# A fused decoder layer: wide GpSimd products go to VectorE, the second norm's scale leaves the up projection, the branch operands are split in steps

## The chip, the cores and the metric

The kernel runs on one core of one Trainium2 chip. The metric is the device time of one execution in microseconds (us). The engines are TensorE (PE in the profile, with its weight loads as PEld), VectorE (DVE), ScalarE (ACT), GpSimd (POOL) and SyncE (SP), whose queue issues nearly all DMA transfers. Each engine runs its own instructions strictly in order and waits on semaphores for the others.

## The reference, cut to what matters

One decoder layer for 1024 prompt tokens and 8 x 4 sample tokens (1056 columns together), width 1024, all float32:

```
xn = rms_norm(x, norm1_g)
z  = xn @ w_in                       # q, k, v and gates of three mixers, and three branch gates
o_a, o_b, o_c = GLA scan, FoX attention, HGRN2 scan   # o_a and o_c: rms_norm(o) * silu(gate)
merged = sum_b sigmoid(g_b) * (o_b @ w_branch_b)
x  = x + merged @ w_out
h  = rms_norm(x, norm2_g)
x  = x + (silu(h @ w_ffn_gate) * (h @ w_ffn_up)) @ w_ffn_down
y  = rms_norm(x, final_norm_g)       # rms_norm(x, g) = x * rsqrt(mean(x*x) + EPS) * g
```

States of the two scans and the new attention keys and values are outputs too.

## The kernel before

Activations lie with features on the 128 partitions and the 1056 columns along the free dimension. So a "wide" tile is 128 x 1056 (528 KB). Each float32 operand of a matmul is split into a rounded part and its remainder (`x` and its subtracted low part, `wh` and `wl`): ACT writes the rounded part (L110, L223), DVE subtracts (L111, L224), and PE multiplies three of the four combinations.

The stages, in the order of the trace: the first norm (0 to 85 us); the input projection in pairs of feature rows by seven products each with 264-column matmuls (L1914; 85 to 690), where the FoX attention runs in the background; the rest of the input projection with 352-column matmuls (L139; to about 985), where the two scans run in the background; 24 branch jobs (to about 1150), in the order FoX, GLA, HGRN2, eight rows each; eight output jobs (to 1250); the up projection `ffn_up` in 22 pairs (to 1700); the down projection (to 1900) and the last norm.

Background work is a set of Python generators in four queues (`bg3`, `bgs`, `bg4`, `bgn`). `tick` is called after every third matmul of a job and advances one queue by one step, in turn. `drain` runs queues to their end. All of this only decides the order in which instructions are written; the compiler's scheduler may then move instructions of one engine past each other where data allow it.

A branch job `n` (0 to 23) loads its gate from DRAM (`z_dram`), ACT applies the sigmoid (L1591), PE multiplies four operand tiles in three column chunks of 12 matmuls each, and DVE multiplies each chunk by the gate (L1596 for the first eight, L1598 after them). Three PSUM banks (`pg`) take the chunks in turn, so PE can be three chunks ahead of DVE. From the ninth job on POOL adds the chunk into `merged` (L1599). Two things stand between these jobs. `ranges`, written ahead of job number `AHEAD`, drains the background queues and tests a flag in an `If` (L1536, L1537) that every engine passes; its body recomputes the scans in another way and isn't executed here. Behind it the four scan outputs for the next eight jobs are fetched (`fetch_o`) and split, two in front of each of the next two jobs (`halves`).

`head_norm` (L1112 to L1133) normalises a scan's output of one head: an Ln and an Exp on ACT (L1116, L1117), three DVE instructions of a Newton step, one product by the head's scale, one by the gate (L1130, on POOL).

In `ffn_up` an even pair is the gate projection `z`, an odd pair the up projection `y`. `post` computes `z*r1`, the sigmoid `g`, `g*r1`, `z*g` and `y*z` (L1972), where `r1` is the second norm's factor for each column; of each two tiles the first is on DVE and the second on POOL. `r1` comes from `rstd`, called as a whole in the first pair. The weights of each pair are added and split by DVE (L1804 to L1808, L224), and chunks leave PSUM by ACT (L1925) or DVE (L1923).

Of the kernel before, what the change touches and what calls it, by code (L numbers as in the profile page):

```python
# [8 lines left out]
F32 = mybir.dt.float32  # L9
# [12 lines left out]
CW = 352  # L22
# [18 lines left out]
AHEAD = 5  # L41
# [49 lines left out]
class Body:  # L91
    def __init__(self, nc, tc, A, O):
        self.nc, self.tc, self.A, self.O = nc, tc, A, O

        self.bg, self.bg3, self.bg4, self.bgs, self.bgn = [], [], [], [], []
        self.turn = 0
        self.early = []
# [131 lines left out]
    def rstd(self, out, sqs, scale, n=NT):  # L229
# [3 lines left out]
        for sl in self.chunks():  # L233
            sl = slice(sl.start, min(sl.stop, n))
            w = sl.stop - sl.start
            ps = self.pm.get()
            for i, sq in enumerate(sqs):
                nc.tensor.matmul(ps[:, :w], self.ones, sq[:, sl], start=i == 0, stop=i == len(sqs) - 1)
            nc.vector.tensor_scalar(v[:, sl], ps[:, :w], scale, EPS, ALU.mult, ALU.add)
            self.pm.put(ps)  # L240
        yield
        nc.scalar.activation(t[:, :n], v[:, :n], AF.Ln)
        nc.scalar.activation(out[:, :n], t[:, :n], AF.Exp, scale=-0.5)
        for sl in self.chunks():
            sl = slice(sl.start, min(sl.stop, n))
            self.newton(out[:, sl], v[:, sl], t[:, sl])
        self.u.put(v, t)
# [32 lines left out]
    def run(self):  # L280
# [17 lines left out]
        self.lf_dram = dp.tile([4, NT], F32, name="lf_dram")  # L298

# [251 lines left out]
    def in_pairs(self, job, nxt):  # L551
# [13 lines left out]
        def post(n, y):  # L565

            name = PAIRS[2 * n][0]
            e = nc.vector, nc.gpsimd
# [9 lines left out]
            for i in range(2):  # L578
                if name == "gq":
                    nc.vector.scalar_tensor_tensor(y[i], y[i], 0.125, self.r1, ALU.mult, ALU.mult)  # L580
                else:
                    e[i].tensor_tensor(y[i], y[i], self.r1, ALU.mult)  # L582
            yield
            yield
            if name in ("gr", "hq", "hg"):
                for i in range(2):
# [3 lines left out]
                    e[i].tensor_tensor(y[i], y[i], g, ALU.mult)  # L590
# [507 lines left out]
    def head_norm(self, o, gate, gn, dst, done):  # L1098
# [17 lines left out]
        nc.scalar.activation(t[:, :n], v[:, :n], AF.Ln)  # L1116
# [13 lines left out]
        nc.gpsimd.tensor_tensor(o[:, :n], o[:, :n], v, ALU.mult)  # L1130
# [114 lines left out]
    def scan_mul(self, hf, q, k, qe, ke):  # L1245
        nc = self.nc
        tt = slice(hf * 512, hf * 512 + 512)
        nc.gpsimd.tensor_tensor(ke, ke, k[:, tt], ALU.mult)
        nc.gpsimd.tensor_tensor(qe, qe, q[:, tt], ALU.mult)
# [168 lines left out]
    def scan_sample(self, q, k, b, vn, hs, os, s0_src, sts_out, done):  # L1418
# [77 lines left out]
        nc.gpsimd.tensor_tensor(S0, S0, ebl, ALU.mult)  # L1496
# [54 lines left out]
    def out_jobs(self, last):  # L1551
# [32 lines left out]
        def branch_job(n):  # L1584
            bi, f = order[n]

            def begin():
# [3 lines left out]
                self.sig = nc.scalar.activation(gates[n], gates[n], AF.Sigmoid)  # L1591

            def evac(ps, c, sl):
# [3 lines left out]
                else:  # L1597
                    nc.vector.tensor_tensor(g[:, sl], ps, g[:, sl], ALU.mult)  # L1598
                    nc.gpsimd.tensor_tensor(mg[:, sl], mg[:, sl], g[:, sl], ALU.add)  # L1599
# [32 lines left out]
        held = []  # L1632

        def ranges():
# [3 lines left out]
            held[:] = fetch_o(0)  # L1638

        def halves(bi, h0):  # L1640
            for h in (h0, h0 + 1):
                split_o(bi, h, held[h])
# [39 lines left out]
    def wout_jobs(self, M):  # L1682
# [24 lines left out]
        def end(f, hh, xf):  # L1707
# [3 lines left out]
            else:  # L1711
                nc.scalar.activation(xf, hh, AF.Square)
                nc.gpsimd.tensor_tensor(self.r1, self.r1, xf, ALU.add)
# [164 lines left out]
    def pair_run(self, nxt, phase, post, hook, into=None, beside=None):  # L1878
# [15 lines left out]
        for n in range(self.pairs):  # L1894
# [3 lines left out]
            y = into(n) if into else [self.u.get(), self.u.get()]  # L1898
# [60 lines left out]
            if post:  # L1959
                assert not pend  # L1960
                steps = post(n, y)
                if steps is not None:
                    next(steps)
                    pend.append(steps)
# [5 lines left out]
    def ffn_up(self, job, nxt):  # L1970
        nc = self.nc
        TT = lambda e, o, x, y, op=ALU.mult: e.tensor_tensor(o, x, y, op)  # L1972
        V, P = nc.vector, nc.gpsimd
# [3 lines left out]
        def phase():  # L1977
            self.close("o")
            f = self.open("f", "right", reuse_waits="tile")
            self.u = Slots(f, 6, [128, NT], F32, "fu")  # L1980
# [6 lines left out]

        def hook(n, k):
            if n == 0 and k == 1:
                for _ in self.rstd(self.r1, [self.r1], 0.125):  # L1990
                    pass
            if n < N - 1:
                return

            if k == 1:
# [9 lines left out]
            elif k == 6:  # L2005
                for j in range(2):
                    take(loads.pop(0))

# [322 lines left out]
```

## Time and profile before

| | us |
|---|---|
| median of 3 runs (lowest to highest) | 1962.71 (1962.51 to 1969.71) |
| the profiled execution | 1971.27 |
| its span in the trace | 1969.5 |
| mean granted TensorE clock, share of full speed | 0.987 |

The profile is of an execution of its own, a little longer than the three timed ones; 1.8 us lie outside its span. Its rows give when an instruction started, how long it took, and what ended the idle time in front of it. "PEclk" is the share of full speed that the clock of TensorE was granted in a stretch; its two levels are 0.5 (1.2 GHz) and 1.0 (2.4 GHz), and a value between them is a mean.

### The profile page before, as it was taken

What the parts mean: (1) busy time and instruction counts of PE and PEld (TensorE: products, weight loads), DVE (VectorE), ACT (ScalarE), POOL (GpSimd) and SP (SyncE); (2) the same over time, 40 slices, a digit from 0 to 9 for tenths busy, and PEclk for the clock granted to TensorE, in tenths of its full rate; (3) what the DMA queues carried; (4) which work ended last, traced back from release to release, by engine and by line L of the source; (5) the groups of instructions that cost most, each with busy time, mean ns of one, the idle gap of its engine ahead of it and who ended that gap; (6) DMA issues with size and microseconds to landing.
All of it is one profiled execution on the core that took longest, in us unless ns stands there. A gap on an engine that the chain in (4) does not pass through costs nothing. (4 is left out here: it accounts for less than half of the span.)

```text
span 1969.5 us, 37117 instructions
## 1 busy us (share of the span) xinstructions
PE 1909.6 (97%) x14846; PEld 1818.4 (92%) x14846; DVE 1338.5 (68%) x2205; ACT 826.0 (42%) x1464; POOL 463.5 (24%) x295
## 2 busy tenths in 40 slices
PE   8999999999999999999989999999999999999997
PEld 6889999999999988888889999999999999999896
DVE  8866556644666577786565555977677777668965
ACT  5444444322433354454544423633334333332435
POOL 5211011211222132122113522222223222110004
PEclk9999999999999999999999999999999999999998
DMA  3433433577666534343446443122221221423212
GB/s 145 150 128 113 155 102 94 157 235 239 191 207 204 179 109 143 121 144 122 144 151 223 147 148 114 62 76 99 76 76 66 77 99 52 175 87 110 85 60 88
DMA packets 96983, 253.60 MB, mean 129 GB/s; under 512 B 14562, under 2 KB 28066, under 8 KB 96802
## 3 DMA queue, kind: packets, MB, share of 16 engines
q1 hardware_dynamic: 95250, 249.96, 37.3%
q8 instruction: 118, 1.93, 0.4%
q10 hardware_dynamic: 1296, 0.67, 0.1%
q14 instruction: 63, 0.52, 0.1%
q0 software_dynamic: 256, 0.52, 0.1%
HBM read 183.74 MB, written 67.37 MB: 127 GB/s over the span
## 5 line engine op out<-in xcount | busy, mean ns | idle before, releaser
L139 PE MATMUL pg<-x,wh 128*128 128x352 f32 x1692 | 431.3, 336 | 9.2 <-DVE u L1596 7.2
L1914 PE MATMUL pg<-x,wh 128*128 128x264 f32 x2080 | 400.1, 288 | 8.1 <-POOL frmul L773 2.7
L1914 PEld LDWEIGHTS pg<-x,wh 128*128 128x128 f32 x2080 | 322.9, 188 | 14.7 <-POOL x L224 2.9
L139 PEld LDWEIGHTS pg<-x,wh 128*128 128x128 f32 x1692 | 297.4, 191 | 31.4 <-issue 14.7
L1914 PE MATMUL pg<-x,wl 128*128 128x264 f32 x1040 | 295.7, 284 | 0.4 <-DVE wl L224 0.4
L139 PE MATMUL pg<-x,wl 128*128 128x352 f32 x846 | 277.4, 328 | 1.4 <-PEq L1537 1.4
L1914 PEld LDWEIGHTS pg<-x,wl 128*128 128x128 f32 x1040 | 195.7, 188 | 0.6 <-DVE wl L224 0.6
L1914 PE MATMUL pg<-x,rh 128*128 128x264 f32 x976 | 187.3, 288 | 2.3 <-DVE fu L1923 2.3
L139 PEld LDWEIGHTS pg<-x,wl 128*128 128x128 f32 x846 | 162.2, 192 | 2.2 <-issue 2.2
L1914 PE MATMUL pg<-pr,wh 128*128 128x264 f32 x832 | 162.5, 293 | 0.0
L1914 PEld LDWEIGHTS pg<-x,rh 128*128 128x128 f32 x976 | 152.4, 190 | 4.0 <-DVE fu L1923 2.7
L224 DVE TENSOR_TENSOR wl<-wf,wh 128x512 fp32r<-128x512 f32 (+2 forms) x125 | 108.6, 870 | 54.0 <-ACT wh L223 50.3
L223 ACT ACTIVATE wh<-wf 128x512 fp32r<-128x512 f32 (+2 forms) x125 | 77.5, 620 | 153.4 <-PE pg L1914 120.7
L1914 PE MATMUL pg<-x,rl 128*128 128x264 f32 x488 | 139.2, 285 | 0.0
L1914 PEld LDWEIGHTS pg<-pr,wh 128*128 128x128 f32 x832 | 129.9, 190 | 4.7 <-issue 3.1
L582 POOL TENSOR_TENSOR pu<-pu,r 128x1056 f32<-128x1056 f32 x21 | 59.0, 2809 | 312.1 <-ACT pu L1925 312.1
L1914 PE MATMUL pg<-pr,wl 128*128 128x264 f32 x416 | 118.8, 286 | 0.0
L1972 POOL TENSOR_TENSOR fu<-fu,r 128x1056 f32<-128x1056 f32 x22 | 67.1, 3048 | 216.1 <-ACT fu L1925 202.9
L110 ACT ACTIVATE wh<-wf 128x1024 fp32r<-128x1024 f32 (+2 forms) x60 | 51.3, 855 | 151.2 <-PE pg L139 135.9
L1914 PEld LDWEIGHTS pg<-x,rl 128*128 128x128 f32 x488 | 92.4, 189 | 0.0
L1923 DVE TENSOR_TENSOR pu<-pu,pg 128x264 f32<-128x264 f32 x132 | 55.3, 426 | 53.4 <-PE pg L1914 52.1
L1925 ACT ACTIVATE pu<-pg 128x264 f32<-128x264 f32 x176 | 66.3, 381 | 58.8 <-PE pg L1914 54.0
(510 smaller groups left out, 4371.0 us busy)
## 6 DMA issues: line engine op xcount, KB each, us to landing
z_dram<-pu SPq DMA_DIRECT2D x44, 528.0 KB
wf<-in_wgu SPq DMA_DIRECT2D x44, 512.0 KB
u<-z_dram SPq DMA_DIRECT2D x39, 528.0 KB
wf<-in_winp SPq DMA_DIRECT2D x30, 512.0 KB
fa<-in_kc SPq DMA_DIRECT2D x48, 256.0 KB
fa<-in_vc SPq DMA_DIRECT2D x48, 256.0 KB
wf<-in_win SPq DMA_DIRECT2D x19, 512.0 KB
a_dram<-fu SPq DMA_DIRECT2D x18, 528.0 KB
```

Source lines behind the costliest of these rows:

```text
L110: nc.scalar.activation(wh[:, :n], wf[:, :n], AF.Copy)
L139: nc.tensor.matmul(ps[:m, :CW], a[:, k, :], b[:, sl], start=n == 0, stop=n == 3 * job.kt - 1)
L223: nc.scalar.activation(h, x, AF.Copy)
L224: (eng or nc.vector).tensor_tensor(l, x, h.bitcast(F32), ALU.subtract)
L582: e[i].tensor_tensor(y[i], y[i], self.r1, ALU.mult)
L1914: nc.tensor.matmul(ps, a[:, w], b, start=first and m == 0, stop=m == 3 * K - 1, skip_group_check=not first)
L1923: nc.vector.tensor_tensor(out, out, ps, ALU.add)
L1925: nc.scalar.activation(out, ps, AF.Copy)
L1972: TT = lambda e, o, x, y, op=ALU.mult: e.tensor_tensor(o, x, y, op)
```

## The change

1. Wide element products and sums that POOL executed go to DVE: the input projection's norm product and sigmoid product (L582 x21, L590 x6), the gate product of `head_norm` (L1130 x8), the scans' decay products (L1248 and L1249 x12 each) and state product (L1496 x6), the branch sum (L1599 x48), the sum of squares (L1713 x7), all of `post` in `ffn_up` (L1972 x43) and the differences of the down projection (L2070 x6, L2082 x6).
2. The up projection is no longer multiplied by `r1`: `g*r1` (44 products) is gone. Instead the residual `h` is divided by it. `rstd_2` loads each of the eight `h` tiles from DRAM in the background of `ffn_up`, multiplies it by `v*r1` (which is 1/r1) and stores it, and it stores `EPS*v` (`v_dram`), which the last norm adds in place of `EPS`. The Newton step works on whole tiles, and the second norm's steps come one per product of the up projection.
3. `fetch_o` and the splits of the branch operands become `load_o`, a generator in `bgn`: it fetches four tiles, waits eight steps, and splits one tile per step. `drain` in front of jobs 8 and 16 finishes it. `AHEAD` goes from 5 to 6, and `tick` skips one call after each step when only one queue holds work.
4. `head_norm` asks for the table set of Ln and Exp once (`tables`) when a sigmoid has been issued since.
5. In the last up pair `y*z` and its split are spread over the last products; `ffn_up` has 8 buffers in place of 6, the down projection 14 in place of 13.

```diff
-AHEAD = 5
+AHEAD = 6
...
     def tick(self):
         qs = self.bg3, self.bgs, self.bg4, self.bgn
-        for _ in () if self.cold else qs:
-            q = qs[self.turn % 4]
+        if self.cold or not any(qs):
+            return
+        if self.pause:
+            self.pause -= 1
+            return
+        while not qs[self.turn % 4]:
             self.turn += 1
-            if q:
-                self.pump(q)
-                return
+        self.pump(qs[self.turn % 4])
+        self.turn += 1
+        self.pause = max(0, 2 - sum(map(bool, qs)))
...
+    def rstd_2(self):
+        nc = self.nc
+        v, t = self.u.get(), self.u.get()
+        for sl in self.chunks():
+            ps = self.pm.get()
+            nc.tensor.matmul(ps[:, :CW], self.ones, self.r1[:, sl], start=True, stop=True)
+            nc.vector.tensor_scalar(v[:, sl], ps[:, :CW], 0.125, EPS, ALU.mult, ALU.add)
+            self.pm.put(ps)
+            yield
+        r = self.r1
+        nc.scalar.activation(t, v, AF.Ln)
+        nc.scalar.activation(r, t, AF.Exp, scale=-0.5)
+        yield
+        nc.vector.scalar_tensor_tensor(t, v, -0.5, r, ALU.mult, ALU.mult)
+        nc.vector.tensor_tensor(t, t, r, ALU.mult)
+        nc.vector.scalar_tensor_tensor(r, t, 1.5, r, ALU.add, ALU.mult)
+        yield
+        self.inv = t
+        nc.vector.tensor_tensor(t, v, r, ALU.mult)
+        nc.scalar.activation(v, v, AF.Copy, scale=EPS)
+        nc.sync.dma_start(self.v_dram, v)
+        self.u.put(v)
+        yield
+        for f in range(8):
+            h = self.u.get()
+            nc.sync.dma_start(h, self.h_dram[f])
+            for _ in range(5):
+                yield
+            nc.vector.tensor_tensor(h, h, t, ALU.mult)
+            yield
+            yield
+            nc.sync.dma_start(self.h_dram[f], h)
...
-        nc.scalar.activation(t[:, :n], v[:, :n], AF.Ln)
+        ln = nc.scalar.activation(t[:, :n], v[:, :n], AF.Ln)
+        if self.tab is None:
+            self.tab = self.tables(self.sig)
+            self.follow(ln, self.tab)
         nc.scalar.activation(r[:, :n], t[:, :n], AF.Exp, scale=-0.5)
...
-        nc.gpsimd.tensor_tensor(o[:, :n], o[:, :n], v, ALU.mult)
+        nc.vector.tensor_tensor(o[:, :n], o[:, :n], v, ALU.mult)
...
         def ranges():
             self.drain(self.bg3, self.bg4, self.bgs, self.bgn)
             self.any_range([t for t in merged if t is not None])
-            held[:] = fetch_o(0)
+            self.bgn.append(load_o(0, 8))
+        def load_o(bi, wait):
+            ts = fetch_o(bi)
+            for _ in range(wait):
+                yield
+            for h, t in enumerate(ts):
+                split_o(bi, h, t)
+                yield
...
             if n == AHEAD:
                 yield ranges
             elif n == 12:
-                yield lambda: held.__setitem__(slice(None), fetch_o(2))
-            for bi, at in ((0, AHEAD + 1), (2, 13)):
-                for i in range(2):
-                    if n == at + i:
-                        yield lambda bi=bi, i=i: halves(bi, 2 * i)
+                yield lambda: self.bgn.append(load_o(2, 8))
+            elif n in (8, 16):
+                yield lambda: self.drain(self.bgn)
...
             if n % 2 == 0:
                 z[:] = y
                 for i in range(2):
-                    TT(e[i], z[i], z[i], self.r1)
+                    TT(V, z[i], z[i], self.r1)
+                yield
                 g = [self.u.get(), self.u.get()]
                 for i in range(2):
                     nc.scalar.activation(g[i], z[i], AF.Sigmoid)
+                yield
                 for i in range(2):
-                    TT(e[i], g[i], g[i], self.r1)
-                for i in range(2):
-                    TT(e[i], z[i], z[i], g[i])
+                    TT(V, z[i], z[i], g[i])
...
-        self.nc.gpsimd.tensor_tensor(e[:, b], e[:, b], e[:, a], ALU.subtract)
+        self.nc.vector.tensor_tensor(e[:, b], e[:, b], e[:, a], ALU.subtract)
...
-        P.tensor_tensor(o[:, a], o[:, a], e[:, b], ALU.subtract)
+        V.tensor_tensor(o[:, a], o[:, a], e[:, b], ALU.subtract)
...
-            nc.vector.tensor_scalar(v[:, :w], ps[:, :w], 0.125, EPS, ALU.mult, ALU.add)
+            nc.vector.scalar_tensor_tensor(v[:, :w], ps[:, :w], 0.125, self.r1[:, sl], ALU.mult, ALU.add)
```

The order of instructions on an engine shows where the `If` falls among the branch jobs. On DVE before, `pg_95`, `pg_91` and `pg_96` are the three banks, `wl_73` and `wl_74` the two weight buffers of the jobs, and L1536 and L1537 the `If`:

```order
L1596 TENSOR_TENSOR u_8248<-pg_95,u_8247 128x352
L111 TENSOR_TENSOR wl_74<-wf_70,wh_72 128x512
L1596 TENSOR_TENSOR u_8248<-pg_91,u_8247 128x352
L1596 TENSOR_TENSOR u_8248<-pg_96,u_8247 128x352
L111 TENSOR_TENSOR wl_73<-wf_69,wh_71 128x512
L1536 TENSOR_LOAD rg_f
L1537 COMPARE_AND_BRANCH
```

The three chunks here are of job 4, and the two weight splits of jobs 5 and 6; PE's own `If` stands behind the fifth matmul of job 5. The same place on DVE in the changed kernel, where L1627 is the product with the gate, L1152 to L1161 the last `head_norm`, and L1567 and L1568 the `If`:

```order
L111 TENSOR_TENSOR wl_73<-wf_69,wh_71 128x512
L1152 SCALAR_TENSOR_TENSOR u_8249<-u_8253,u_8248 128x1056
L1627 TENSOR_TENSOR u_8246<-pg_91,ub_8274 128x352
L1154 TENSOR_TENSOR u_8249<-u_8249,u_8248 128x1056
L1627 TENSOR_TENSOR u_8246<-pg_96,ub_8274 128x352
L1157 SCALAR_TENSOR_TENSOR u_8248<-u_8249,u_8248 128x1056
L111 TENSOR_TENSOR wl_74<-wf_70,wh_72 128x512
L1159 SCALAR_TENSOR_TENSOR ub_8271<-ub_8271,c_hng,u_8248 128x1056
L1161 TENSOR_TENSOR ub_8271<-ub_8271,u_8253 128x1056
L111 TENSOR_TENSOR wl_73<-wf_69,wh_71 128x512
L1567 TENSOR_LOAD rg_f
L1568 COMPARE_AND_BRANCH
```

The chunks here are the last two of job 5; the weight splits are of jobs 6, 7 and 8. PE's `If` now stands behind all 36 matmuls of job 6, whose three chunks DVE takes only behind the `If`, and the last weight split in front of it overwrites the buffer that job 6 reads. Behind the `If` ACT's queue of the changed kernel begins thus, where `wf_70` is the raw weight of job 9 and `x_83` to `x_89` are the four operands that job 8 needs:

```order
L1622 ACT_TABLE_LOAD
L1622 ACTIVATE ub_8276<-ub_8276 128x1056
L227 ACTIVATE x_83<-ub_8275 128x1056
L227 ACTIVATE x_85<-ub_8273 128x1056
L110 ACTIVATE wh_72<-wf_70 128x512
L227 ACTIVATE x_87<-ub_8270 128x1056
L227 ACTIVATE x_89<-ub_8272 128x1056
```

And SP's queue at that place, which issues the transfers:

```order
L1613 DMA ub_8276<-z_dram_212 128x1056
L1600 DMA ub_8275<-o_dram_99 128x1056
L1600 DMA ub_8273<-o_dram_100 128x1056
L1600 DMA ub_8270<-o_dram_101 128x1056
L1600 DMA ub_8272<-o_dram_102 128x1056
L1613 DMA ub_8277<-z_dram_197 128x1056
L1613 DMA ub_8274<-z_dram_198 128x1056
L1613 DMA ub_8271<-z_dram_199 128x1056
L1613 DMA u_8249<-z_dram_200 128x1056
L109 DMA wf_70<-in_wbr 128x512
```

Before, the four `o_dram` loads came first, then three gates, then a weight; the gate of job 6 (`z_dram_211`) was behind the four loads, and is now loaded ahead of the `If`.

## Rows read from the trace of the kernel before

**Rows 1.** the page: busy time of each engine, share of the span, instructions.

```profile
PE 1909.6 (97%) x14846; PEld 1818.4 (92%) x14846; DVE 1338.5 (68%) x2205; ACT 826.0 (42%) x1464; POOL 463.5 (24%) x295
```

**Rows 2.** waits of PE: total us, times, longest us.

```profile
PE pg L139 <- DVE u L1596: 7.2, 2, 4.1
PE pg L1914 <- DVE fu L1923: 3.2, 2, 2.3
PE pg L1914 <- ACT fu L1925: 2.8, 1, 2.8
PE pg L1258 <- POOL h L1249: 1.5, 1, 1.5
PE pg L139 <- PEq L1537: 1.4, 1, 1.4
PE pg L238 <- DVE fu L239: 1.4, 1, 1.4
```

**Rows 3.** windows: us; PE, PEld, DVE, ACT, POOL busy; PEclk; DMA share; GB/s.

```profile
1016.60:1024.00 7.40, 7.37 (x28) 7.37 (x29) 5.85 (x8) 0.63 (x1) 2.44 (x1) 0.58 0.43 142
1044.90:1052.00 7.10, 7.07 (x29) 7.07 (x30) 2.58 (x5) 3.95 (x5) 0.00 (x0) 0.63 0.80 287
1286.00:1291.00 5.00, 5.00 (x31) 5.00 (x32) 3.09 (x7) 1.08 (x3) 0.00 (x0) 0.69 0.62 220
1690.90:1697.00 6.10, 6.10 (x40) 6.10 (x39) 3.27 (x5) 2.50 (x4) 0.00 (x0) 0.72 0.55 187
```

**Rows 4.** groups by line, POOL: busy us, mean ns | idle before.

```profile
L582 POOL TENSOR_TENSOR pu<-pu,r 128x1056 f32<-128x1056 f32 x21 | 59.0, 2809 | 312.1 <-ACT pu L1925 312.1
```

**Rows 5.** timeline, first pair of the up projection: start us, us.

```profile
1268.06 1.25 DVE L1972 TENSOR_TENSOR fu<-fu,r 128x1056 f32<-128x1056 f32 x1
...
1274.06 3.60 POOL L1972 TENSOR_TENSOR fu<-fu,r 128x1056 f32<-128x1056 f32 x1 [1.20 <-ACT fu L2017]
1275.22 2.98 DVE L1807 TENSOR_TENSOR st<-wf,st 128x512 f32<-128x512 f32 x1
1278.13 3.51 DVE L1972 TENSOR_TENSOR fu<-fu,fu 128x1056 f32<-128x1056 f32 x1
```

**Rows 6.** timeline of ACT, end of the up projection.

```profile
1690.00 0.67 ACT L1925 ACTIVATE fu<-pg 128x264 f32<-128x264 f32 x2 [3.42 <-POOL fu L1972]
```

**Rows 7.** timeline, DVE and POOL in the down projection.

```profile
1834.63 0.70 DVE L2080 TENSOR_TENSOR du<-du,du 128x528 f32<-128x528 f32 x1
...
1835.47 1.32 POOL L2082 TENSOR_TENSOR du<-du,du 128x528 f32<-128x528 f32 x1 [56.15 <-DVE du L2080]
1835.59 1.76 DVE L2081 TENSOR_TENSOR du<-du 128x528 f32<-128x528 f32 x1
```

**Rows 8.** timeline of DVE, branch jobs, with the idle time before.

```profile
1014.60 1.55 DVE L1121 SCALAR_TENSOR_TENSOR ub<-u,ub 128x1056 f32<-128x1056 f32 x1 [2.08 <-ACT ub L1117]
...
1031.79 0.53 DVE L1596 TENSOR_TENSOR u<-pg,u 128x352 f32<-128x352 f32 x1 [3.10 <-DVEq L1537]
```

**Rows 9.** timeline of ACT in the same jobs.

```profile
1027.33 0.63 ACT L110 ACTIVATE wh<-wf 128x512 fp32r<-128x512 f32 x1 [6.43 <-PE pg L139]
1035.59 1.09 ACT L223 ACTIVATE x<-u 128x1056 fp32r<-128x1056 f32 x1 [7.63 <-DMA u<-o_dram]
...
1041.94 1.28 ACT L1591 ACT_TABLE_LOAD   x1 [0.31 <-DMA ub<-z_dram]
1043.24 3.03 ACT L1591 ACTIVATE ub<-ub 128x1056 f32<-128x1056 f32 x3
```

**Rows 10.** windows of whole stages, columns as in the third group.

```profile
100.00:690.00 590.00, 584.53 (x5372) 551.25 (x5372) 352.66 (x682) 236.09 (x509) 102.57 (x75) 1.00 0.51 168
1050.00:1150.00 100.00, 100.00 (x618) 99.83 (x617) 57.60 (x79) 38.56 (x43) 54.25 (x48) 1.00 0.42 141
1300.00:1675.00 375.00, 375.00 (x3084) 375.00 (x3083) 280.04 (x350) 142.76 (x291) 103.83 (x36) 1.00 0.22 76
1840.00:1858.00 18.00, 15.46 (x111) 13.87 (x110) 18.00 (x34) 6.22 (x11) 2.63 (x2) 1.00 0.31 97
```

More of the change, by code (lines that the diff above doesn't have):

```diff
@@ L233, in rstd @@
         for sl in self.chunks():
-            sl = slice(sl.start, min(sl.stop, n))
-            w = sl.stop - sl.start
             ps = self.pm.get()
-            for i, sq in enumerate(sqs):
-                nc.tensor.matmul(ps[:, :w], self.ones, sq[:, sl], start=i == 0, stop=i == len(sqs) - 1)
-            nc.vector.tensor_scalar(v[:, sl], ps[:, :w], scale, EPS, ALU.mult, ALU.add)
+            nc.tensor.matmul(ps[:, :CW], self.ones, self.r1[:, sl], start=True, stop=True)
+            nc.vector.tensor_scalar(v[:, sl], ps[:, :CW], 0.125, EPS, ALU.mult, ALU.add)
             self.pm.put(ps)
+            yield
+        r = self.r1
+        nc.scalar.activation(t, v, AF.Ln)
+        nc.scalar.activation(r, t, AF.Exp, scale=-0.5)
         yield
-        nc.scalar.activation(t[:, :n], v[:, :n], AF.Ln)
[L243 to L247, printed above, removed]
+        nc.vector.scalar_tensor_tensor(t, v, -0.5, r, ALU.mult, ALU.mult)
[17 more added lines that the diff above has]
+            nc.sync.dma_start(self.h_dram[f], h)
+            self.u.put(h)
+            for _ in range(4):
+                yield
+        self.u.put(t)
     def tables(self, after):
@@ L1962, in pair_run @@
                 if steps is not None:
-                    next(steps)
-                    pend.append(steps)
+                    if next(steps, "end") != "end":
+                        pend.append(steps)
         for steps in pend:
@@ L1986, in take @@
             self.u.put(t)
+        norm = self.rstd_2()
         def hook(n, k):
-            if n == 0 and k == 1:
-                for _ in self.rstd(self.r1, [self.r1], 0.125):
-                    pass
+            if n or k:
+                next(norm, None)
             if n < N - 1:
                 return
+            y = self.y
             if k == 1:
@@ L2004, in hook @@
                     self.rfree(hl)
-            elif k == 6:
+            elif k == 4:
                 for j in range(2):
                     take(loads.pop(0))
+            elif k == 5:
+                TT(V, y[0], y[0], z[0])
+                take(y[0])
+            elif k == 6:
+                TT(V, y[1][:, HC:NT], y[1][:, HC:NT], z[1][:, HC:NT])
         def post(n, y):
-            e = V, P
             if n % 2 == 0:
@@ L2017, in post @@
                     nc.scalar.activation(g[i], z[i], AF.Sigmoid)
+                yield
                 for i in range(2):
-                    TT(e[i], g[i], g[i], self.r1)
-                for i in range(2):
-                    TT(e[i], z[i], z[i], g[i])
+                    TT(V, z[i], z[i], g[i])
                 self.u.put(*g)
                 return
-            for i in range(2):
-                TT(V if n == N - 1 else e[i], y[i], y[i], z[i])
-                if n == N - 1:
-                    take(y[i])
-                elif n == N - 3:
+            if n == N - 1:
+                TT(V, y[1][:, 0:HC], y[1][:, 0:HC], z[1][:, 0:HC])
+                take(y[1])
+                self.u.put(*z)
+                return
+            for i in range(2):
+                TT(V, y[i], y[i], z[i])
+            self.u.put(*z)
+            yield
+            for i in range(2):
+                if n == N - 3:
                     held.append(y[i])
@@ L2055, in phase_d @@
             nc.sync.dma_start(self.h[f], self.h_dram[f])
-        self.raws = u.free + [self.r1]
+        self.raws = u.free
+        nc.sync.dma_start(self.r1, self.v_dram)
         d = self.open("d2", "right", reuse_waits="tile")
```

38 lines of the change are left out of this document (16 added, 22 removed).

## The prediction

> **What bounds the kernel now.** I read the page first. PE is busy for 1909.6 of 1969.5 us [rows 1], so everything that a change can give lies in the 60 us in which PE stands still, and in slower matmuls behind such a stop. DVE, at 1338.5 us, has some 630 us to spare on average, which says nothing about any one place.
>
> Second, PE's list of waits [rows 2]. The reader is to see which are ended by an engine that this change touches: 7.2 us for the branch chunks on DVE (twice, the longest 4.1, so the other 3.1); 3.2 and 2.8 us in the up projection, of which one stop of 2.3 is early and one of 2.8 at its end; 1.5 us for a scan product on POOL; 1.4 us each at the `If` and in the second norm.
>
> Third, the granted clock behind the stops [rows 3]. PE is busy throughout these stretches, yet the clock means 0.58, 0.63, 0.69 and 0.72, a mixture of 0.5 (1.2 GHz) and 1.0 (2.4 GHz). The share missing times the busy time is what a stop costs once more: 0.42 x 7.37 = 3.1 us, 0.37 x 7.07 = 2.6, 0.31 x 5.0 = 1.6 and 0.28 x 6.1 = 1.7.
>
> Fourth, the timeline where POOL and DVE work at once. The same product of two 128x1056 tiles took 1.25 us on DVE alone, and 3.51 us beside a product on POOL; a 512-wide sum took 2.98 us beside a POOL product that itself took 3.60 [rows 5]. In the down projection a 528-wide product took 0.70 us alone and one of the same width 1.76 us, beginning 0.12 us behind a POOL product of 1.32: it ends 0.56 us after POOL does [rows 7]. So a wide POOL instruction stops DVE for as long as it lasts.
>
> **The change part by part.** *Products from POOL to DVE.* A wide product costs 1.25 us on DVE [rows 5] against a mean of 2.81 on POOL [rows 4], during which DVE's own work is stopped. In the 375 us of the up projection's middle DVE is busy 280 us with POOL at 104, and PE never waits [rows 10]. POOL's 36 instructions there are nine each of four products. Nine `g*r1` are gone, 27 go to DVE, and DVE loses nine of its own: 18 x 1.25 = 22 us more. The eight rescaled `h` tiles add 10 us and 16 transfers at a DMA share of 0.22. What hides these 32 us is the 95 us that DVE has free there, and what it no longer waits for POOL; without that cover they would count whole. I take 0. In the input projection 27 products (21 in [rows 4], and six sigmoid products) add 34 us to 353 of 590; cover 237 us; 0, bounds +3 and -3, since single waits may move either way. The 48 branch sums, 0.53 us each on DVE as the chunk's own product takes [rows 8], add 25 us to 58 of 100 [rows 10], where PE does not wait: 0.
>
> *First pair of the up projection.* PE waits 2.3 us for DVE's next chunk [rows 2]. In the run of DVE work in front of it two instructions are stretched, by 3.51 - 1.25 = 2.3 and 2.98 - 0.7 = 2.3 us (a 528-wide one takes 0.70) [rows 5, 7]. The change takes these 4.6 us out and puts two products, 2.5 us, in: the run is 2.1 us shorter, and the stop nearly vanishes, with its 1.6 us of clock. Gain 3.8, bounds 0 and 4.
>
> *Second norm.* Its 1.4 us for the chunk's evacuation [rows 2] came from three matmuls at once; now one per product. Gain 1.0, bounds 0 and 1.4.
>
> *End of the up projection.* PE waits 2.8 us for ACT, which had waited 3.42 us for POOL's last product [rows 2, 6]. The product becomes 1.25 us on DVE and most of the last pair's work is moved ahead. Gain 2.8 + 1.7 of clock = 4.5; bounds 2 and 5.
>
> *Scan products.* The wait of 1.5 us on POOL [rows 2]: the DVE product starts behind another DVE instruction, so I take 1.0, bounds 0 and 1.5, more if the clock stays up.
>
> *Down projection.* At 1840 us DVE is busy in 18.00 of 18 us and PE in 15.46 [rows 10]. Three times a 528-wide pair, 1.76 on DVE beside 1.32 on POOL, becomes two of about 0.63 (0.70 at most): 0.4 to 0.5 us each. Gain 1.5, bounds 0 and 2.
>
> *Last norms of the scans.* At 1016 us DVE stood 2.08 us in a Newton step that waits for ACT's Exp [rows 8], with a chunk behind it that PE needed: 3.1 us, and 3.1 of clock. In the new order the Newton step of the last norm stands behind the first chunk of job 5, and the norms come further apart. Gain 5.7, bounds 0 and 6.2. That tables are loaded once I count at nothing. By the order on ACT the last norms' Ln and Exp still have a load each, as a sigmoid comes between, and a load takes 1.28 us, with the next instruction 0.02 us behind it [rows 9]. The Trainium skill, "ScalarE: Activation LUTs", section "What ACT_TABLE_LOAD costs", gives 1.283 us for the load, and 1.38 more to drain at each switch. The first agrees with the row; of the second the row shows nothing. Were one load saved in front of that Exp, the sum would gain up to 1.28 us more by the row and 2.66 by the page.
>
> *The `If`.* Here the change costs. Before, DVE stood 3.10 us at the `If` [rows 8], but PE, five matmuls into job 5 and with free banks, lost only 1.4 [rows 2]. Now all of job 6 stands ahead of PE's `If` and its three chunks behind DVE's, so PE has no bank until DVE is through; and DVE's last weight split in front of it overwrites what job 6 reads, so it starts when job 6 ends. From that end, T: copy 0.63, split as long, `If` 3.1, chunk 0.53 = 4.9 us until PE goes on. Queued behind the waiting split on DVE are the `If` and all chunks. Then job 8 needs four fetched tiles. The first landed 3.8 us after DVE's `If` (1035.59 - 1031.79), four more by 1041.94, 1.6 us apiece [rows 8, 9]. SP now brings a gate, four tiles, four gates and then the weight of job 9, and ACT has that weight's copy in front of the last two operands. That is landing at T + 3 + 3.8 + 8 x 1.6 + 0.8 = T + 20.4, and copy, operand copy 1.09 and subtract 1.25 make T + 23.3. PE gets there at T + 4.9 + 5.8 (36 matmuls at 100 us / 618 [rows 10]) + 1 for half of a chunk, and about 3 for a lowered clock: T + 14.7. So it waits up to 8.6 us more, and 2.6 of clock follow. Together 4.9 + 3 + 8.6 + 2.6 = 19.1 against 1.4 + 4.1 + 2.6 = 8.1 now: loss 11. If SP is through its `If` at T and the transfers run a fifth faster, the second wait is about 2.5 and the loss 5. I take 8; what was late before, the gate of job 6 behind four tiles, is no longer late.
>
> Sum: 3.8 + 1.0 + 4.5 + 1.0 + 1.5 + 5.7 - 8 = 9.5 gained, call it 10. Against the profiled execution: 1971.3 - 10 = 1961. That execution is 8.6 us over the median of the runs, so the median becomes 1952.7.
>
> **The rivals.** *The splits come in time.* If the background steps keep PE fed behind the `If` as they do elsewhere, only the 4.9 us and its clock remain, no worse than now: 17 us gained, 1945. For it: the transfers there moved the five tiles in 6.4 us [rows 9]. Against it: the written order on ACT. Chance 0.2.
>
> *The gains are eaten.* The stop at the `If` costs the full 11, and the norms' stop only changes place, as table loads still stand ahead of each Exp: 3.8 + 1.0 + 4.5 + 1.0 + 1.5 - 11 = 1 gained, 1962. For it speaks the same order. Chance 0.25.
>
> *DVE becomes the bound: slower.* Where DVE has no idle time, each moved instruction counts whole: the down projection and the first pairs, at 18.00 of 18 us [rows 10], show the state. Were the scans' stage and the up projection's middle to reach it, at a load of up to 280 + 32 of 375 us, in bursts of four products (5 us) between chunks, each of 22 pairs would stop PE by about 1 us, 22 in all, against 10 gained: 1975. It decides from the point where a burst outlasts the banks. Against it: DVE now holds runs with instructions stretched to 3 us, and PE does not wait in those 375 us [rows 5, 10]. Chance 0.13.
>
> The Trainium skill bears on this one ("Perfetto Trace Analysis", "Optimizing Scalar/DVE Operations"): with DVE saturated, moving work to GpSimd may make sense, though it might not help as they share a port. By its first half this change would lose in the down projection; by rows 7 DVE waits for POOL there anyway, and by them it gains.
>
> **How the numbers follow.** The likeliest case, gains as summed with 8 lost at the `If`, gets 0.42, and its own range is 1947 to 1958. 1945 has 0.2, 1962 has 0.25, 1975 has 0.13. A change of under 0.5% (9.8 us) can't be told from none here; so faster means below 1952.9. The likeliest case lies on that edge and gives half of its chance to each side, 0.21; with 0.2 from the first rival and the part of the second that ends lower, 0.04, faster has 0.46. Same has 0.21 + 0.21 of the second + 0.01 = 0.41, and slower 0.13. The range 1939 to 1970 takes in the first two rivals with the bounds of their terms and leaves out most of the slower one.
>
> **What would show it.** After: no DVE instruction beside POOL above 1.4 us for a wide product; no wait of PE on `fu` L1925 or L1923 counterparts above 1 us; a PE stop of about 5 us at the `If`, and another in job 8 that ends with ACT's copies of operands behind a weight's copy; no stop at the last norms. I am wrong if PE passes the `If` in under 2 us, or if waits on DVE appear in the middle of the up projection.

## The result and the profile after

| | before | after |
|---|---|---|
| median (lowest to highest), us | 1963.28 (1962.51 to 1969.71) | 1937.35 (1936.83 to 1938.65) |
| profiled execution, us | 1971.27 | 1937.29 |
| its span, us | 1969.5 | 1935.5 |
| mean granted TensorE clock | 0.987 | 0.993 |

The ratio is 0.9862, 95% interval 0.984 to 0.9883: 26 us faster, where 10 were forecast and the range ended at 1939.

The page of the changed kernel, the row that answers to [rows 1]:

```profile
PE 1897.3 (98%) x14846; PEld 1808.2 (93%) x14846; DVE 1331.9 (69%) x2362; ACT 835.3 (43%) x1467; POOL 107.6 (6%) x120
```

The same 14846 matmuls keep PE busy for 1897.3 us in place of 1909.6, and PE stands still for 1935.5 - 1897.3 = 38.2 us in place of 59.9. So of the 34 us between the two profiled executions 21.7 are stops that went and 12.3 are time in which the same matmuls ran slower, most of it at a lowered clock. POOL is down from 463.5 to 107.6 us. DVE has 157 instructions more and is busy for 7 us less.

PE's waits after (the view of [rows 2]: us in total, times, longest):

```profile
PE pg L139 <- DVE u L1627: 6.8, 1, 6.8
...
PE pg L1946 <- DVE du L1955: 2.1, 5, 0.8
PE pg L879 <- DVE fa L871: 1.5, 2, 1.1
...
PE pg L1946 <- DVE fu L1955: 0.2, 1, 0.2
```

Of the waits in [rows 2] those for the second norm, for ACT at the end of the up projection, for POOL's scan product, and nearly all of those for `fu` (L1923 before, L1955 after) are gone. One branch wait of 6.8 us stands where there were 7.2 and 1.4.

Whole stages after (the columns of [rows 3] and [rows 10]: us; PE, PEld, DVE, ACT, POOL busy; PEclk; DMA share; GB/s):

```profile
100.00:690.00 590.00, 587.75 (x5397) 554.96 (x5398) 365.45 (x725) 242.05 (x517) 30.93 (x51) 1.00 0.52 171
1290.00:1665.00 375.00, 375.00 (x3083) 375.00 (x3082) 250.09 (x371) 149.74 (x295) 0.00 (x0) 1.00 0.27 94
```

The reader is to compare the last row with its counterpart in [rows 10]. In 375 us of the up projection DVE is busy 250 us where it was 280, although by the prediction's count the change put 32 us of products there. So an estimate of what POOL had cost DVE by stopping it is 280 + 32 - 250 = 62 us. DVE's instructions of the same stretches, one by one, bear it out. Before, for example:

```profile
L1805 DVE TENSOR_TENSOR st<-st,wf 128x512 f32<-128x512 f32 x18 | 32.8, 1824 | 0.3
```

The same sum takes 0.69 us on average after (L1837, shown with the experiments). The sum in front of it went from 2.03 to 0.69, and two kinds of weight split from 0.92 and 1.01 to 0.69; times their numbers that makes 65 us. In the input projection PE was idle for 590 - 584.5 = 5.5 us and is now for 2.3.

**How much of 34 is the profile.** The two medians are 26 us apart, the two profiles 34. A second profile of the kernel before (1964.3 us, span 1962.5) shows PE's long waits at the same places. Two differ in length: the one at the `If` is 2.5 us and not 1.4, the one at the gate behind it 2.6 and not 4.1. Its page row is

```profile
PE 1903.4 (97%) x14846; PEld 1812.3 (92%) x14846; DVE 1337.7 (68%) x2205; ACT 825.4 (42%) x1464; POOL 464.8 (24%) x295
```

PE stands still for 59.1 us there (59.9 in the first), but it is busy 6.2 us less, again for the same matmuls. Its stretches behind the four stops of [rows 3], with the same columns:

```profile
1012.60:1020.00 7.40, 7.37 (x36) 7.37 (x37) 7.09 (x9) 0.63 (x1) 2.46 (x1) 0.77 0.44 142
1040.70:1047.80 7.10, 7.10 (x36) 7.10 (x37) 2.53 (x5) 3.89 (x5) 0.00 (x0) 0.80 0.78 280
1280.80:1285.80 5.00, 5.00 (x44) 5.00 (x43) 3.69 (x6) 1.70 (x4) 1.20 (x1) 1.00 0.62 216
1684.00:1690.30 6.30, 6.30 (x41) 6.30 (x41) 3.50 (x6) 2.68 (x4) 0.00 (x0) 0.73 0.56 187
```

The clock means 0.77, 0.80, 1.00 and 0.73, where the first profile has 0.58, 0.63, 0.69 and 0.72. So the first profile was an execution in which the clock stayed low for longer behind the same stops, and my clock terms, 9 us together there, were 0.23 x 7.37 + 0.20 x 7.1 + 0 + 0.27 x 6.3 = 4.8 in this one. Against this second profile the changed kernel's span is 27.0 us shorter, 20.9 of it stops that went and 6.1 time in which matmuls ran slower; that is close to the 26 us between the medians.

### The profile page after: what moved, and what is told of

Same layout as the page of the kernel before. It is cut to its first block, busy times and chain, and to the rows that moved or that the text cites. A ratio compares the mean times of both kernels' runs of the same rounds, so it can differ in the third digit from the quotient of the medians.

```text
span 1935.5 us, 36932 instructions
## 1 busy us (share of the span) xinstructions
PE 1897.3 (98%) x14846; PEld 1808.2 (93%) x14846; DVE 1331.9 (69%) x2362; ACT 835.3 (43%) x1467; POOL 107.6 (6%) x120
## 5 line engine op out<-in xcount | busy, mean ns | idle before, releaser
L228 DVE TENSOR_TENSOR wl<-wf,wh 128x512 fp32r<-128x512 f32 (+2 forms) x125 | 88.3, 707 | 48.4 <-ACT wh L227 44.9
L1955 DVE TENSOR_TENSOR fu<-fu,pg 128x264 f32<-128x264 f32 x132 | 56.2, 428 | 66.8 <-PE pg L1946 66.5
L1955 DVE TENSOR_TENSOR pu<-pu,pg 128x264 f32<-128x264 f32 x132 | 55.9, 426 | 67.0 <-PE pg L1946 66.2
L1957 ACT ACTIVATE fu<-pg 128x264 f32<-128x264 f32 x176 | 66.9, 384 | 63.2 <-PE pg L1946 63.1
```

Source lines behind the costliest of these rows:

```text
L228: (eng or nc.vector).tensor_tensor(l, x, h.bitcast(F32), ALU.subtract)
L1955: nc.vector.tensor_tensor(out, out, ps, ALU.add)
L1957: nc.scalar.activation(out, ps, AF.Copy)
```

## The experiments

All times are compared with runs of the kernel before on the same chip; their medians lay between 1964.9 and 1967.2 us. Theory 1 was that wide POOL instructions stop DVE and come late themselves, and that most stops of PE came from that; theory 2 that the written order gains.

| kernel | median, us | ratio to before (95%) |
|---|---|---|
| moves_only | 1946.1 | 0.9888 (0.9873 to 0.9904) |
| no_moves | 1957.3 | 0.9951 (0.9937 to 0.9965) |
| moves_inproj | 1959.1 | 0.9966 (0.9952 to 0.9979) |
| moves_scans | 1963.3 | 0.9990 (0.9980 to 1.0001) |
| moves_rest | 1954.1 | 0.9939 (0.9924 to 0.9953) |
| idle_pool | 2022.1 | 1.0275 (1.025 to 1.0299) |
| idle_timed | 1950.8 | 0.9933 (0.9913 to 0.9953) |
| order_undone | 1941.4 | 0.9871 (0.9848 to 0.9894) |
| ahead5 | 1940.2 | 0.9866 (0.9839 to 0.9892) |
| no_pause | 1940.0 | 0.9864 (0.9837 to 0.9891) |
| tables_undone | 1936.7 | 0.9844 (0.9826 to 0.9862) |
| banks6 | 1936.2 | 0.9857 (0.9838 to 0.9877) |
| banks6_ahead5 | 1939.2 | 0.9871 (0.9853 to 0.9890) |

**before_again.** The kernel before, unchanged, one profile; read above.

> The kernel before, unchanged, for a second profile. The first profiled execution took 1971.3 us, 8 over the median of its runs. If that execution had stops of PE that most executions do not have, this profile shows 1963 +- 1 us and some of the stops listed before are missing or shorter, together by about 8 us with the clock behind them; if the stops are the same in all, the difference is spread evenly and each stage is about 0.4% shorter.

In sum the stops were the same (59.1 and 59.9 us) and the time was 7 us less, but not spread evenly: PE's busy time is 6.2 us longer in the first, and 4.2 of them lie behind the four stops shown above.

**moves_only.** The kernel before with every product that the change moves:

```diff
-            e = nc.vector, nc.gpsimd
+            e = nc.vector, nc.vector
...
-        nc.gpsimd.tensor_tensor(o[:, :n], o[:, :n], v, ALU.mult)
+        nc.vector.tensor_tensor(o[:, :n], o[:, :n], v, ALU.mult)
...
-        V, P = nc.vector, nc.gpsimd
+        V, P = nc.vector, nc.vector
```

> The kernel before with all the wide POOL products of the change put on DVE, g*r1 kept (its second half too on DVE), nothing else changed. Theory 1 (wide POOL instructions stop DVE and come late themselves, and that is what most stops of PE came from): most of the 26 us gained, 1940 to 1946 us, and the stops at 171, 267, 319, 360, 698, 892, 1286 and 1690 us gone. Theory 2 (the written order gains: the pause in tick, AHEAD, the splits in steps, the steps of the second norm and of the last pair): at most 8 us gained, 1955 to 1963, as DVE has the same or more to do in the same order.

It gained 1.1%, some 22 us, and the stops named went or fell to 0.5 us and less (the longest at 264 us). That is at the edge of what theory 1 said. Most of the time that PE stands still beyond that of the whole change (43.0 us against 38.2) lies among the branch jobs:

```profile
PE pg L139 <- DVE u L1596: 8.8, 2, 5.1
...
PE pg L139 <- PEq L1537: 1.6, 1, 1.6
```

The stop at the last norm, 3.1 us before, is 5.1 here, with 3.7 at the gate behind the `If` and 1.6 at the `If`. That these stops are what its time lacks is not shown: order_undone, below, has nearly the same ones at a ratio of 0.9871.

**no_moves.** The changed kernel with those products on POOL again (in `post`, `e = V, nc.gpsimd` as before; the other lines likewise).

> The changed kernel with every product that the change put on DVE back on POOL where it still exists; all of the rest of the change kept. Theory 1: 1953 to 1961 us, the stops in the input projection and the scans are back. Theory 2: 1937 to 1945 us.

It gained 0.5%. Theory 1 says 1953 to 1961, theory 2 at most 1945, so most of the gain goes with the moves. The 0.5% that is left belongs to the other parts of the change together. Of these, the up projection without `g*r1` and the spread work of its last pair were not undone by themselves; the first of them also takes products from POOL. The waits of the input projection (`fa`, `fs`) and of the scans (L1281 is the scan product on POOL, L1294 the wait at 892 us) are back:

```profile
PE pg L139 <- DVE u L1628: 7.4, 1, 7.4
...
PE pg L880 <- DVE fa L872: 2.8, 3, 1.6
...
PE pg L880 <- DVE fs L854: 2.4, 2, 1.2
PE pg L1290 <- POOL h L1281: 2.1, 2, 1.5
PE pg L1237 <- DVE at L1294: 1.8, 1, 1.8
```

**moves_inproj, moves_scans, moves_rest.** The moves in three parts: `e = nc.vector, nc.vector` in the input projection alone; the scans' three products and the one of `head_norm`; all others.

> The kernel before with only the 27 products of the input projection (norm product and sigmoid product) on DVE. Theory 1: the four stops of PE at 171, 267, 319 and 360 us (5.5 us together) go, 1956 to 1959 us. Theory 2: no difference beyond 2 us, and the stops stay, since the attention's own chain sets them.

> The kernel before with only the scans' products (decay, state, and the gate product of head_norm) on DVE. The stops at 698 (1.7 us, waiting for POOL) and at 892 us (2.0 us, DVE late) should go and the clock with them: 3 to 6 us gained. If DVE's stop there had nothing to do with POOL, only the 1.7 us at 698 go: 1 to 2 us gained.

> The kernel before with the remaining moves only: branch sums, sum of squares, post of the up projection, differences of the down projection. All moves together gained 1.1%, those of the input projection 0.34%, those of the scans 0.1%. If the parts add up, this gains 0.65 to 0.75% (13 to 15 us), with the stops at 1286 and 1690 us gone. If the parts help each other (a stop removed in one stage is given back in the next, as the scans' was at the last norm), it gains under 0.5%.

The ratios fall short of 1 by 0.34, 0.10 and 0.61%, together 1.05 against 1.12 for all at once: the parts add up. Two of the input projection's four stops went and two shrank to 0.5 and 0.4 us, as theory 1 said. PE's waits on the attention before, and then with the moves (in both, one of 1.1 us for `fa`, at 99 us, is none of these four):

```profile
PE pg L851 <- DVE fa L843: 2.9, 3, 1.6
PE pg L851 <- DVE fs L825: 2.1, 2, 1.1
PE pg L864 <- DVE fs L825: 1.1, 1, 1.1
```

```profile
PE pg L851 <- DVE fa L843: 1.4, 2, 1.1
PE pg L851 <- DVE fs L825: 0.5, 1, 0.5
```

The scans' part missed what I expected. The stops at 698 and 892 us went (1.5 us, in [rows 2], and 1.8, the first line below, of before), and the time hardly changed; the other two lines are of moves_scans:

```profile
PE pg L1205 <- DVE at L1262: 1.8, 1, 1.8
```

```profile
PE pg L139 <- DVE u L1596: 6.9, 2, 5.1
...
PE pg L139 <- PEq L1537: 1.9, 1, 1.9
```

The stop at the last norm is 5.1 us where it was 3.1, but the one at the gate behind the `If` is 1.8 where it was 4.1: with the `If` the branch jobs lose 8.8 us, and lost 8.6 (8.2 in the second profile of before). So the scans' 3.3 us were not given back there as a whole. PE stands still for 57.6 us in all, where the second profile of before has 59.1; what took the rest back is not shown. moves_rest fell a little short of the 0.65% expected, and its stops at 1286 and 1690 us went but for 0.3 us.

**idle_pool.** Does a POOL product cost by coming late, or by stopping DVE? The changed kernel with products that nobody reads:

```diff
+            for q in range(4):
+                nc.gpsimd.tensor_tensor(self.idle, self.r1[:, q * 176:q * 176 + 176], self.r1[:, q * 176:q * 176 + 176], ALU.mult)
...
                     TT(V, z[i], z[i], self.r1)
+                TT(nc.gpsimd, self.idle, self.r1, self.r1)
+                TT(nc.gpsimd, self.idle, self.r1, self.r1)
...
                 TT(V, y[i], y[i], z[i])
+            TT(nc.gpsimd, self.idle, self.r1, self.r1)
+            TT(nc.gpsimd, self.idle, self.r1, self.r1)
```

> The changed kernel with idle GpSimd products added: in the input projection four products of 176 columns of r1 into a scratch tile behind each product of post, in the up projection two 1056-wide products of r1 behind each z*r1 and each y*z. Nobody reads the scratch tiles. Theory 1a (a wide POOL instruction stops DVE, whoever needs its result): DVE instructions beside them stretch to 2.5 us or more, stops of PE come back in the input projection and in the first pair of the up projection, 1943 to 1950 us. Theory 1b (the gain was that the products themselves end earlier; the stretching mattered little): 1936 to 1939 us.

It cost some 81 us against the changed kernel by the two ratios (85 by the medians, which were not taken beside each other), far more than the 6 to 13 that I expected of theory 1a. As nothing holds these products back, POOL ran them in two bursts and not spread as meant. First the changed kernel, then this one, in 100 us of the up projection (columns as above):

```profile
1290.00:1390.00 100.00, 100.00 (x824) 100.00 (x823) 67.38 (x102) 39.41 (x80) 0.00 (x0) 1.00 0.28 98
```

```profile
1290.00:1390.00 100.00, 58.72 (x374) 57.15 (x374) 96.56 (x60) 18.15 (x37) 91.19 (x38) 0.77 0.18 65
```

With POOL busy for 91 of 100 us, DVE is busy for 97 where it was for 67, and executes 60 instructions in place of 102; PE has 374 matmuls in place of 824. DVE's 512-wide subtracts, 0.69 us in the changed kernel, took on average here (for one kind; us in total and ns of one behind the bar):

```profile
L228 DVE TENSOR_TENSOR rl<-st,rh 128x512 fp32r<-128x512 f32 x5 | 11.8, 2362 | 0.0
```

**idle_timed.** The same question at a rate nearer to the old one: one idle product behind each sigmoid, where `g*r1` had been. These are 22, in a stage where POOL had executed 43 before. (The change took out 22 `g*r1`, eleven of them on POOL, and not 44.)

```diff
                     nc.scalar.activation(g[i], z[i], AF.Sigmoid)
+                    TT(nc.gpsimd, self.idle, g[i], self.r1)
```

> The changed kernel with one idle 1056-wide GpSimd product behind each sigmoid of the up projection (sigmoid by r1 into a scratch tile that nobody reads), 22 in all, at the time when g*r1 stood before. Theory 1a: DVE instructions beside them stretch from 1.25 to 2.5 us or more; in the first pair a stop of PE of 1 to 3 us comes back, in the middle none, as PE does not wait for DVE there: 1938 to 1942 us. Theory 1b: no instruction stretches, 1936 to 1938 us.

Slower than the changed kernel by 0.7% (13 us), more than the 1 to 5 of theory 1a. PE's waits on `fu` came back, 4.3 us for DVE and 1.4 for ACT, at both ends of the stage (for DVE at 1262 and 1675 us) and not in its middle. These 5.7 us and a clock lowered behind the last of them are what the profile shows; it is of the shortest of the four executions. The product `z*r1` on DVE in the changed kernel and here, with the idle one on POOL (ns, least, median, largest):

```profile
L2004 DVE TENSOR_TENSOR fu<-fu,r x22: 1249/1251/1253, 1249.5 to 1656.0; 128x1056 f32<-128x1056 f32 x22
```

```profile
L2004 DVE TENSOR_TENSOR fu<-fu,r x22: 1250/1254/3540, 1247.5 to 1659.5; 128x1056 f32<-128x1056 f32 x22
L2004 POOL TENSOR_TENSOR idle<-fu,r x22: 2823/3478/3497, 1251.4 to 1664.3; 128x1056 f32<-128x1056 f32 x22
```

The median hides that about ten of the 22 were stretched (an estimate: 19 of them, in the middle of the stage, take 46.6 us together, at 1.25 or 3.54 us each). Of all DVE instructions there two kinds changed by much, `z*r1` and L1837. L1837 is shown next to one that did not change, first in the changed kernel and then here:

```profile
L1955 DVE TENSOR_TENSOR fu<-fu,pg 128x264 f32<-128x264 f32 x110 | 47.1, 429 | 63.4 <-PE pg L1946 63.1 <-DMA wf<-in_wgu 0.2
L1837 DVE TENSOR_TENSOR st<-st,wf 128x512 f32<-128x512 f32 x18 | 12.4, 688 | 0.3
```

```profile
L1955 DVE TENSOR_TENSOR fu<-fu,pg 128x264 f32<-128x264 f32 x110 | 45.1, 424 | 37.5 <-PE pg L1946 36.9
L1837 DVE TENSOR_TENSOR st<-st,wf 128x512 f32<-128x512 f32 x18 | 32.9, 1825 | 0.3
```

L1837, with two inputs in SBUF, went from 0.69 to 1.83 us on average, which is what the same sum took before the change (L1805, 1.82). The chunk's evacuation L1955, with one of its inputs in PSUM, stayed at 0.42 to 0.43. So the prediction's "a wide POOL instruction stops DVE" holds here for DVE instructions with both inputs in SBUF. The Trainium skill, "SBUF — State Buffer", section "Who interferes with whom", says the same: a DVE instruction with two SBUF inputs contends with a GpSimd instruction that reads SBUF, and one with at most one, outside the 2-port modes, doesn't. The rows of L1837 and L1955 agree with both halves.

**order_undone, ahead5, no_pause, tables_undone.** Four ways back among the branch jobs: the order as before (`AHEAD` 5, `fetch_o` and `halves`, no pause); `AHEAD = 5` alone; `self.pause = 0` alone; and the three lines of `tables` in `head_norm` taken out.

> The changed kernel with the order among the branch jobs as before: AHEAD 5, the tiles fetched behind the If and split two in front of a job, no pause in tick. Moves, tables and the second norm's steps stay. If the new order is worth what the branch jobs show (16 us of stops and lowered clock with the moves alone, 9 with the whole change): 1942 to 1946 us, with stops at the last norms, at the If and at the gate behind it. If it is worth nothing by itself: 1936 to 1939.

> The changed kernel with AHEAD 5 alone. If the place of the If only moves the one stop of 7 us: 1936 to 1939 us. If the sixth job is what gives the spread norms time to end before the drain: a stop at the last norm comes back ahead of the If, 1940 to 1945 us.

> The changed kernel with the pause in tick taken out. If the pause is what parts the last norm's instructions from the chunks: a stop of 2 to 5 us at the last norm and a lowered clock behind it, 1940 to 1945 us; and the four splits of load_o come twice as early, before their tiles land, so a wait on a tile's transfer ahead of job 8. If not: 1936 to 1939 us.

> The changed kernel without the request for the table set in head_norm. The changed kernel executed 26 table loads, the one before 24. If the request does nothing for the last norms, as forecast: 24 to 27 loads, and 1936 to 1939 us. If it saves loads in front of the Exps: a stop at the last norm comes back, 1939 to 1943 us.

None differs from the change by more than the intervals, with ratios of 0.9871, 0.9866, 0.9864 and 0.9844 against 0.9862. order_undone shows the stops again that it was to show:

```profile
PE pg L139 <- DVE u L1627: 8.5, 3, 5.1
...
PE pg L139 <- PEq L1568: 1.5, 1, 1.5
```

These are 8.5 and 1.5 us where the change has 6.8, so the order is worth some 3 us of stops in one profile, and its 2 to 4 us of time are inside what these runs can tell. ahead5 lies at the edge between its two cases; its profiled execution took 8372 us, and no stops are read from it. With `AHEAD` 6 and no pause a stop of 5.1 us at the last norm came back, as expected, and one of 0.8 us for an operand behind the `If`; the ratio is the change's all the same. The table request has no share in the gain: the table loads are 24 before, 26 with it, and 24 again without it. The last norms (L1144 is the Ln, L1148 the Exp) have with it:

```profile
L1144 ACT ACT_TABLE_LOAD x3 | 3.8, 1283 | 0.1
L1148 ACT ACT_TABLE_LOAD x3 | 3.8, 1283 | 0.1
```

**banks6, banks6_ahead5.** An attempt at the one stop that is left: `self.banks(6)` behind `any_range`, which gives the jobs behind the `If` three more PSUM banks; and the same with `AHEAD = 5`.

> The changed kernel with three more PSUM banks for the jobs behind the If, so that job 7 need not wait for DVE to take job 6's chunks. If the stop of 7 us at the If is for banks, as the order says: it shrinks to 1.5 to 3 us. If the next limit is the fetched tiles of job 8 (last one split at 1040 us in the changed kernel), a stop of 3 to 5 us appears there instead, and the time stays within 2 us, 1935.5 to 1938; if not, 1930 to 1933 us.

> The same with AHEAD 5, so that two jobs stand between the If and job 8 and cover the fetch. If the fetch limits: no stop in job 8, but a stop at the last norm ahead of the If, as the norms have one job less to end in: 1932 to 1937 us. If the norm's stop costs as much as it does with AHEAD 5 in the written order (5.3 us): 1937 to 1940.

Neither beats the change clearly. In banks6 the profile puts PE's wait no longer down to a chunk, but to DVE at the `If`:

```profile
PE pg L139 <- DVEq L1568: 5.2, 1, 5.2
```

The stop shrank from 6.8 to 5.2 us, not to 1.5 to 3, so free banks are the smaller part of it: 1.6 us at most, and DVE itself was held at the `If` for 4.1 us there and for 5.0 in the changed kernel. What PE needs from DVE there, if not a bank, isn't shown. With `AHEAD` 5 the same stop is 7.4 us, and neither of the two cases expected came.

## Why the prediction was wrong

**Failed: the loss of 8 at the `If`.** The step was "landing at T + 3 + 3.8 + 8 x 1.6 + 0.8": I took the weight whose copy stands in front of the last two operands on ACT to be the one that SP loads behind nine transfers. In the changed kernel T, the end of job 6, is 1020.0. SP's issues of branch weights:

```profile
1017.30 0.33 SPq L109 DMA_DIRECT2D wf<-in_wbr  x1
...
1021.43 0.33 SPq L109 DMA_DIRECT2D wf<-in_wbr  x1
...
1038.78 0.33 SPq L109 DMA_DIRECT2D wf<-in_wbr  x1
```

ACT there:

```profile
1020.05 0.63 ACT L110 ACTIVATE wh<-wf 128x512 fp32r<-128x512 f32 x1 [5.19 <-PE pg L139]
...
1032.79 1.09 ACT L227 ACTIVATE x<-ub 128x1056 fp32r<-128x1056 f32 x1
1034.13 1.09 ACT L227 ACTIVATE x<-ub 128x1056 fp32r<-128x1056 f32 x1 [0.26 <-DMA ub<-o_dram]
1035.13 0.61 ACT L110 ACTIVATE wh<-wf 128x512 fp32r<-128x512 f32 x1
```

The copy at 1035.13 waits for nothing, and the load it needs had been issued at 1017.30, in front of the `If`; the one behind the nine transfers, at 1038.78, is of a later job. The operands came as they landed, PE had no second stop, and the first rival held. Without the loss of 8 the sum was 17 and the forecast 1945, half of the 16 us by which it fell short. The copies in the order were read rightly; I matched the name of the buffer, `wf_70`, to the wrong one of its loads. The order ahead of the prediction shows only the later load.

**Right in kind, too small: the stop at the `If`.** Forecast 4.9 us, measured 6.8. DVE there:

```profile
1020.71 0.69 DVE L111 TENSOR_TENSOR wl<-wf,wh 128x512 fp32r<-128x512 f32 x1 [0.91 <-ACT wh L110]
1026.42 1.39 DVE L1627 TENSOR_TENSOR u<-pg,u 128x352 f32<-128x352 f32 x3 [5.02 <-SPq L1568]
1032.75 0.96 DVE L1627 TENSOR_TENSOR u<-pg,ub 128x352 f32<-128x352 f32 x2 [4.94 <-ACT ub L1622]
```

The weight split at 1020.71 begins when job 6 has ended, as I said. But then DVE is held for 5.02 us and not 3.10, and the row puts that down to SP's part of the `If`. SP could enter it only when the load at 1021.43 was out, which needed the buffer that this split frees; that makes SP some 0.4 us later than DVE. Why SP then needed until 1026.6, its next transfer, isn't shown. In sum the branch jobs lost 1.4 + 3.1 + 4.1 us in stops before and 6.8 after, and the lowered clock behind them cost 3.1 + 2.6 before and 0.30 x 7 = 2.1 after (PEclk 0.70 from 1027 to 1034 us): a gain of 1.8 + 3.6 = 5.4, where I had the norms' 5.7 less 8. Against the second profile of before, where the three stops make 8.2 us, the gain in stops is 1.4.

**Failed: stages counted at 0.** For the input projection I took 0, "bounds +3 and -3", because DVE had 237 us free. The moves there gained 0.34% alone, 6.7 us. Its four stops ended with a DVE instruction of the attention (`fa`, `fs`), and not with POOL, so I did not ask what had held that instruction up. An average share of free time says nothing about a chain in which DVE is the next step. With every term at its upper bound and no loss at the `If` my sum is 23 us, and there the range ended; the input projection's bound of 3 was wrong, and the scans' second stop had no term.

**Right in kind, mis-sized.** First pair: forecast 3.8, and the wait on `fu` fell from 3.2 in two to 0.2. The second norm's 1.4 and the 2.8 at the end went whole; the end gained another 1 us, the second of the two waits on `fu` in [rows 2]. In the down projection 1.5 was forecast; two waits of before,

```profile
PE pg L1914 <- DVE du L1923: 2.9, 6, 0.7
...
PE pg L1914 <- DVE du L2106: 1.2, 1, 1.2
```

make 2.1 us together after (L1955), 2.0 less. Scan products: 1.0 was forecast for the stop at 698; with the moves the one at 892 went too (in moves_scans, and not in no_moves), which I had in no term.

**Right.** The middle of the up projection: nothing, as PE did not wait before or after; DVE's load there even fell. Tables: still loads for Ln and Exp of the last norms, no effect. No stop at the last norms, as said. The slower rival did not come: in the middle of the up projection DVE is busy 250 of 375 us. In the down projection DVE still has no idle time (18.00 of 18 us from 1806 on), and PE is busy 15.92 us there, against 15.46 in [rows 10].

**A sign that came only in part.** No wide DVE product beside POOL was to take above 1.4 us. In the stages that the change touched no kind of them does on average. In the first norm, which it left as it was, POOL still has wide products, and DVE's take 3.4 us each beside them:

```profile
16.74 10.27 POOL L504 TENSOR_TENSOR su<-su,su 128x1056 f32<-128x1056 f32 x3
```

```profile
17.82 10.32 DVE L231 SCALAR_TENSOR_TENSOR x<-su,g,x 128x1056 fp32r<-128x1056 f32 x3
```

What moving these would be worth was not tried.

**The base.** I took the profiled execution to be 8.6 us slower throughout and subtracted that at the end. It was the clock behind the very stops that the change removes, so it was counted in the terms (9 us of clock, 4.8 in the other profile) and subtracted again. That error of some 4 us went the other way: without it the forecast would have been later still. Two small slips changed nothing: the parts of the chances add up to 0.45 for faster and 0.43 for same, not 0.46 and 0.41, and in the 6.4 us of [rows 9] four transfers landed, not five.

## What to carry to other kernels

Where POOL and DVE both run wide products with their inputs in SBUF, price a POOL product as DVE time too: here some 62 us of DVE's 280 in one stage were waits for POOL (an estimate), and idle POOL products alone cost some 13 and 81 us. An engine's average free time hides this, since it sits in the chains that PE waits for. And when an order is read for what a wait is for, match each buffer's use to its own load by counting the uses, not by the name.

## What was not expected of the hardware

Behind the same stops, of the same length, the granted clock stayed low for very different times in two executions of one kernel: 0.69 against 1.00 in the 5 us behind the stop in the first up pair (2.3 us in both), 0.58 against 0.77 behind the last norm (3.1 us in both). PE's busy time differs by 6 of the 7 us between these executions. The kernel before spreads over 7 us (1962.5 to 1969.7), the changed kernel, with fewer stops, over 1.8 us; that the clock makes this spread too is likely but not shown. Why it fell shorter in one than in the other, these runs don't tell.
